# Both column halves of the mLSTM output projection at hand at once, and its products taken in another order

## The chip, the cores and the metric

One core of a Trainium2 chip runs the whole program. The metric is the device time of one execution in microseconds (us). The engines are PE (TensorE, matrix products), DVE (VectorE), ACT (ScalarE), POOL (GpSimd) and SP (SyncE, which issues most DMAs). They run side by side, each through its own list of instructions in order, and wait for one another by semaphores.

## The reference

A small decoder trunk in float32: 512 tokens of width 1024, one mLSTM layer, then one sliding-window attention layer. Each layer ends with the same three steps. What matters here:

```python
def mlstm_mixer(x, w_in, b_ig, b_fg, head_g, w_out):
    ...
    h = h.reshape(B, S, D_MODEL).astype(x.dtype)
    return (jax.nn.sigmoid(o) * h) @ w_out

    for i in range(DEPTH):
        ...
        x = layer_norm(DEEPNORM_ALPHA * x + mix, mix_ln_g[i], mix_ln_b[i])
        x = layer_norm(DEEPNORM_ALPHA * x + squared_relu_mlp(x, mlp_w_up[i], mlp_w_down[i]), mlp_ln_g[i], mlp_ln_b[i])
        x = x + jax.nn.sigmoid(x @ ple_w_gate[i] + ple_b_gate[i]) * (p[i] @ ple_w_proj[i])
```

The product with `w_out` (1024 x 1024) and the layer norm behind it are the place of the change.

## The kernel before

**Numbers.** Every float32 operand of a product is split into a rounded high part and the rest. `split` (L75) does it: ACT copies the raw tile into `whi` (L76), DVE subtracts to get `wlo` (L77). A product is then three matmuls, high by high, high by low, low by high (`mm3`, L88 to L90).

**Tiling.** The 512 tokens are four tiles of 128, t0 to t3. The width of 1024 is eight k-blocks of 128 on the contracted side and two halves of 512 columns on the output side. One output block (a token tile by a half) takes 8 x 3 = 24 matmuls into one bank of PSUM, the accumulator memory. In this part of the program five banks are called `mm` and three `tp` (for transposes and the small products of the heads).

**Weights.** `load_w` (L79) takes three raw buffers and six pairs `whi`, `wlo` from `wpool`. SP issues the load of a raw tile as soon as DVE has subtracted from the tile that lay there before. Since one half of `w_out` needs four pairs, six pairs hold one half and a part of the next.

**mLSTM.** Four heads follow one another. `mlstm_scores(3)` and `mlstm_out(3)` end with a chain of small steps: products on PE into `tp`, copies on ACT (L414), statistics on DVE, a power on POOL (L138), the scaling of `num` (L428, L431), eight transposes on PE (L435) and the split into `YH`, `YL` (L436, L437). Head 3 fills the last two k-blocks of `YH`, `YL`; k-blocks 0 to 5 are there long before.

**Output projection.** `xstat_mix` (L162) takes half 0 of all four token tiles, then half 1 of all four. Behind each block, `add_res` (L159) adds the scaled residual `res[t]` on DVE and `bn_stats` (L173) takes statistics. Behind half 1 of a token tile comes `ln_finish`: a power on POOL (L138), two passes on DVE over 1024 columns (L145, L146), eight transposes on PE (L129), the split into `XH` on ACT (L133) and `XL` on DVE (L134), and the scaling by alpha on ACT (L149).

**After it.** The first four tiles of the MLP's up projection (L608) take columns 0 to 255 of `XH`, `XL`, so they need token tiles t0 and t1 alone at first. The second layer's output projection (L953 to L966) is code of its own with the same `add_res` and `ln_finish`.

**What sets the order.** The program is written in the order of the source, but the framework's scheduler then simulates the program and sorts each engine's instructions by readiness and priority. So a change at one place can move instructions far behind it as well. The pools reuse memory tile by tile: `mid` (the residual) and the new pool of the change lie partly where the heads' pool `pa` lay.

Of the kernel before, what the change touches and what calls it, by code (L numbers as in the profile page):

```python
# [11 lines left out]
F32R = mybir.dt.float32r  # L12
# [7 lines left out]
P = 128  # L20
S = 512
NT = S // P
D = 1024
KD = D // P
# [21 lines left out]
def yoco_kernel(ctx: ExitStack, tc: tile.TileContext, A: dict, out: bass.AP):  # L46
    nc = tc.nc
    V, ACT, PE, GP = nc.vector, nc.scalar, nc.tensor, nc.gpsimd

    def pool(name, bufs=1, stack=ctx, **kw):  # L50
        return stack.enter_context(tc.tile_pool(name=name, bufs=bufs, **kw))

    base = pool("base")
    wpool = pool("wpool")
# [10 lines left out]
    def mm_bank():  # L65
        return bank("mm")
# [8 lines left out]
    def split(raw, n, hi, lo, eng=V):  # L75
        ACT.copy(hi, raw)  # L76
        eng.tensor_sub(lo, raw, f32(hi))  # L77

    def load_w(src, n, eng=V):  # L79
        raw = wpool.tile([P, 1024], F32, tag="raw", name="wraw", bufs=3)  # L80
        hi = wpool.tile([P, 1024], F32R, tag="whi", name="whi", bufs=6)
        lo = wpool.tile([P, 1024], F32R, tag="wlo", name="wlo", bufs=6)
        nc.sync.dma_start(raw[:, :n], src)
        split(raw[:, :n], n, hi[:, :n], lo[:, :n], eng)
        return hi, lo

    def mm3(o, lh, ll, rh, rl, start, stop):
        PE.matmul(o, lh, rh, start=start, stop=False)  # L88
        PE.matmul(o, lh, rl, start=False, stop=False)  # L89
        PE.matmul(o, ll, rh, start=False, stop=stop)  # L90
# [18 lines left out]
    def tsl(t):  # L109
        return slice(t * P, (t + 1) * P)  # L110
# [29 lines left out]
    def ln_finish(t, st, g, b, mlp_next=True):  # L140
        mv = small.tile([P, 2], F32, tag="mv", name="mv")
        V.bn_aggr(mv, st)
        rs = small.tile([P, 1], F32, tag="rs", name="rs")
        rsqrt_eps(rs, mv[:, 1:2], 1)
        V.scalar_tensor_tensor(res[t], res[t], mv[:, 0:1], g, ALU.subtract, ALU.mult)  # L145
        V.scalar_tensor_tensor(res[t], res[t], rs, b, ALU.mult, ALU.add)  # L146
        transpose_in(res[t], t, XH, XL)
        if mlp_next:
            ACT.mul(res[t], res[t], ALPHA)  # L149
            if t >= 2:  # L150
                r = res[t - 2][:, 512:]
                V.tensor_sub(r, r, res[t][:, 512:])

    def add_res(t, half, ps, alpha):
        r = res[t][:, half * 512:(half + 1) * 512]
        if alpha is None:
            V.tensor_add(r, r, ps)
        else:
            V.scalar_tensor_tensor(r, r, alpha, ps, ALU.mult, ALU.add)  # L159
        return r  # L160

    def xstat_mix(wname, xh, xl, alpha, g, b):  # L162
        sts = [small.tile([P, 2, 6], F32, tag="lst", name="lst", bufs=4) for _ in range(NT)]
        for half in range(2):
            w = [load_w(A[wname][half, c], 1024) for c in range(4)]
            for t in range(NT):
                ps = mm_bank()
                for k in range(KD):
                    wh, wl = w[k // 2]
                    sl = slice((k % 2) * 512, (k % 2 + 1) * 512)  # L170
                    mm3(ps, xh[:, k, tsl(t)], xl[:, k, tsl(t)], wh[:, sl], wl[:, sl], k == 0, k == KD - 1)
                r = add_res(t, half, ps, alpha)
                V.bn_stats(sts[t][:, half, :], r)  # L173
                if half == 1:
                    ln_finish(t, sts[t], g, b)

    sin = base.tile([P, NT, HALF], F32, name="sin")
    cos = base.tile([P, NT, HALF], F32, name="cos")
# [296 lines left out]
    g, b = bcast(A["mix_ln_g"][0]), bcast(A["mix_ln_b"][0])  # L475
# [327 lines left out]
    w = [load_w(A["w_kv"][0, c], 1024) for c in range(4)]  # L803
# [5 lines left out]
    for t in range(NT):  # L809
        ps = proj512(t, w)  # L810
# [109 lines left out]
    w = load_q(0)  # L920
# [125 lines left out]
```

## Time and profile before

| what | value |
|---|---|
| three executions | 1200.96, 1202.63, 1204.96 us, median 1202.63 |
| profiled execution, own time | 1205.24 us |
| its span, first to last instruction | 1203.5 us |
| DVE busy | 877.7 us, 73% of the span |
| ACT busy | 584.4 us, 49% |
| POOL busy | 95.7 us, 8% |
| HBM read | 119.34 MB, 103 GB/s over the span |

The profile is of one execution. A line of its timeline gives start, duration, engine, source line, operation, what is written and read, the shape, the count when several follow one another, and in brackets how long the engine sat idle before it and what ended that wait. The granted clock is the share of full speed that PE was given in a stretch. Times below are counted from the start of the span. The mLSTM's output projection lies at about 168 to 220 us, the attention of the second layer at 650 to 775 us and its output projection at 765 to 800 us.

### The profile page before, as it was taken

How to read it: one execution, taken by the hardware profiler on the slowest of the kernel's cores; microseconds unless marked ns; L12 is line 12 of the kernel's file. 1: busy time of each engine (PE TensorE's matmuls, PEld its weight loads, DVE VectorE, ACT ScalarE, POOL GpSimd, SP SyncE). 2: the span in 40 equal slices, each digit the busy share in tenths (PEclk: the TensorE clock that was granted, in tenths of full speed). 3: DMA queues.
4: the chain of work that ended last, by engine and by line, in shares of the span. 5: the costliest groups of instructions: out<-in, count | busy, mean ns of one | idle time of the engine just before them, and what ended most of it. 6: DMA issues, size and time to landing. Idle time of an engine off the chain costs nothing.

```text
span 1203.5 us, 15661 instructions
## 1 busy us (share of the span) xinstructions
PE 1181.0 (98%) x5918; PEld 1004.2 (83%) x5918; DVE 877.7 (73%) x1454; ACT 584.4 (49%) x1015; POOL 95.7 (8%) x190
## 2 busy tenths in 40 slices
PE   9999999999999999999999999999999999999998
PEld 8899988888888888888788998789888888888877
DVE  6556466877488499599785988586857848959974
ACT  4445551565463463564344655346645536346431
POOL 1011021100000000001201332110000000000100
PEclk9999999999999999999999999989999999999999
DMA  7322227214405316115242211451350440621411
GB/s 229 119 92 71 85 74 280 71 36 140 140 1 179 101 37 192 52 53 175 80 175 88 71 37 36 152 198 36 95 168 18 140 141 1 192 88 36 157 54 52
DMA packets 35995, 124.54 MB, mean 103 GB/s; under 512 B 4096, under 2 KB 4880, under 8 KB 35920
## 3 DMA queue, kind: packets, MB, share of 16 engines
q1 hardware_dynamic: 33840, 116.46, 29.8%
q0 software_dynamic: 2080, 7.09, 1.8%
q8 instruction: 46, 0.75, 0.2%
q14 instruction: 29, 0.24, 0.1%
HBM read 119.34 MB, written 4.19 MB: 103 GB/s over the span
## 4 chain that ended last, share of the span: by engine, by line
PE 88%; DVE 6%; ACT 2%; DMA 2%; issue 1%; SPq 0%; POOL 0%; ACTq 0%; DVEq 0%
PE mm L90 28%; PE mm L89 28%; PE mm L88 28%; PE tp L129 1%; DVE wlo L77 1%; ACT pr L883 1%; ACT whi L76 1%; PE tp L88 1%; PE tp L89 1%; PE tp L90 1%; DMA wraw<-in_w_vo_dram 1%; DVE sc L869 1%; DVE QS L853 0%; DVE smax L870 0%; DMA res<-spill 0%
## 5 line engine op out<-in xcount | busy, mean ns | idle before, releaser
L77 DVE TENSOR_TENSOR wlo<-wraw,whi 128x1024 fp32r<-128x1024 f32 (+1 forms) x168 | 204.2, 1218 | 126.4 <-ACT whi L76 125.4
L76 ACT CAST whi<-wraw 128x1024 fp32r<-128x1024 f32 (+1 forms) x168 | 173.7, 1037 | 243.2 <-PE mm L90 133.1
L89 PE MATMUL mm<-XL,whi 128*128 128x512 f32 (+1 forms) x640 | 237.7, 372 | 1.7 <-DVE XL L134 1.7
L88 PE MATMUL mm<-XH,whi 128*128 128x512 f32 (+1 forms) x640 | 236.2, 371 | 1.9 <-ACT ot L265 1.3
L90 PE MATMUL mm<-XH,wlo 128*128 128x512 f32 (+1 forms) x640 | 237.1, 371 | 0.0
L88 PE MATMUL mm<-whi,XH 128*128 128x512 f32 (+2 forms) x424 | 146.1, 346 | 3.9 <-DVE q L843 2.2
L89 PE MATMUL mm<-wlo,XH 128*128 128x512 f32 (+2 forms) x424 | 145.1, 343 | 0.0
L90 PE MATMUL mm<-whi,XL 128*128 128x512 f32 (+2 forms) x424 | 144.4, 343 | 0.0
L89 PEld LDWEIGHTS mm<-XL,whi 128*128 128x128 f32 x640 | 122.5, 191 | 21.6 <-DVE XL L134 1.9
L88 PEld LDWEIGHTS mm<-XH,whi 128*128 128x128 f32 x640 | 121.6, 191 | 22.3 <-ACT ot L265 1.7
L90 PEld LDWEIGHTS mm<-XH,wlo 128*128 128x128 f32 x640 | 122.5, 191 | 19.9
L76 ACT CAST whi<-rb 128x1024 fp32r<-128x1024 f32 x80 | 84.0, 1051 | 100.6 <-PE mm L89 56.4
L77 DVE TENSOR_TENSOR wlo<-rb,whi 128x1024 fp32r<-128x1024 f32 x80 | 97.6, 1224 | 38.9 <-ACT whi L76 38.9
L88 PEld LDWEIGHTS mm<-whi,XH 128*128 128x128 f32 x424 | 79.9, 189 | 13.0 <-DVE q L843 3.9
L89 PEld LDWEIGHTS mm<-wlo,XH 128*128 128x128 f32 x424 | 80.1, 189 | 7.7 <-issue 1.5
L90 PEld LDWEIGHTS mm<-whi,XL 128*128 128x128 f32 x424 | 80.1, 189 | 6.5 <-issue 0.8
L89 PE MATMUL mm<-wlo,S23h 128*128 128x512 f32 x128 | 50.7, 396 | 0.0
L89 PE MATMUL mm<-wlo,S4Ah 128*128 128x512 f32 x128 | 50.6, 395 | 0.0
L88 PE MATMUL mm<-whi,S23h 128*128 128x512 f32 x128 | 50.6, 395 | 0.0
L88 PE MATMUL mm<-whi,S4Ah 128*128 128x512 f32 x128 | 50.6, 395 | 0.0
L90 PE MATMUL mm<-whi,S4Al 128*128 128x512 f32 x128 | 50.3, 396 | 0.0
L637 DVE TENSOR_TENSOR res<-res,mm 128x512 f32<-128x512 f32 x72 | 48.8, 685 | 1.4 <-PE mm L90 1.0
(354 smaller groups left out, 2231.3 us busy)
## 6 DMA issues: line engine op xcount, KB each, us to landing
wraw<-in_w_up_dram SPq DMA_DIRECT2D x64, 512.0 KB, 3.6
rb<-in_w_down_dram SPq DMA_DIRECT2D x48, 512.0 KB, 4.4
wraw<-in_w_down_dram SPq DMA_DIRECT2D x16, 512.0 KB, 3.5
wraw<-in_w_gate_dram SPq DMA_DIRECT2D x16, 512.0 KB, 3.7
wraw<-in_w_vo_dram SPq DMA_DIRECT2D x18, 412.0 KB, 3.2
wraw<-in_w_qk_dram SPq DMA_DIRECT2D x8, 512.0 KB, 4.7
wraw<-in_w_out_dram SPq DMA_DIRECT2D x8, 512.0 KB, 3.8
wraw<-in_w_q_dram SPq DMA_DIRECT2D x8, 512.0 KB, 3.9
```

The lines of the kernel that those rows point to most:

```text
L76: ACT.copy(hi, raw)
L77: eng.tensor_sub(lo, raw, f32(hi))
L88: PE.matmul(o, lh, rh, start=start, stop=False)
L89: PE.matmul(o, lh, rl, start=False, stop=False)
L90: PE.matmul(o, ll, rh, start=False, stop=stop)
L129: PE.transpose(pt[:, tsl(j)], src[:, tsl(b + j)], ident)
L637: V.tensor_add(r[:, h], r[:, h], bank)
L869: V.copy_predicated(cur, mk, prev)
L883: ACT.activation(pt_[:, par, pr, :], scs[pr][:, par, :], AF.Exp, scale=ASCALE, bias=nm[:, par, pr:pr + 1], accum_out=sm[:, par, pr:pr + 1])
```

## The change

`load_w` can take its `hi` and `lo` tiles from a pool handed to it. `xstat_mix` opens such a pool (`wroom0`, four pairs `xhi`, `xlo`), loads half 0 into `wpool` and half 1 into the new pool, and then goes through the eight blocks in a list of its own: half 0 of t0, t1, t2, then half 1 of t0 and t1, half 0 of t3, half 1 of t2 and t3. The loads, splits and matmuls are the same in number and shape.

```diff
-    def load_w(src, n, eng=V):
+    def load_w(src, n, room=None):
         raw = wpool.tile([P, 1024], F32, tag="raw", name="wraw", bufs=3)
-        hi = wpool.tile([P, 1024], F32R, tag="whi", name="whi", bufs=6)
-        lo = wpool.tile([P, 1024], F32R, tag="wlo", name="wlo", bufs=6)
+        hi, lo = (room.tile([P, 1024], F32R, tag=f"x{x}", name=f"x{x}", bufs=4) if room else
+                  wpool.tile([P, 1024], F32R, tag=f"w{x}", name=f"w{x}", bufs=6) for x in ("hi", "lo"))
         nc.sync.dma_start(raw[:, :n], src)
-        split(raw[:, :n], n, hi[:, :n], lo[:, :n], eng)
+        split(raw[:, :n], n, hi[:, :n], lo[:, :n])
         return hi, lo
...
-        for half in range(2):
-            w = [load_w(A[wname][half, c], 1024) for c in range(4)]
-            for t in range(NT):
-                ps = mm_bank()
-                for k in range(KD):
-                    wh, wl = w[k // 2]
...
+        wctx = ExitStack()
+        room = pool("wroom0", stack=wctx, side="right", reuse_waits="tile")
+        w = [[load_w(A[wname][half, c], 1024, room if half else None) for c in range(4)] for half in range(2)]
+        for t, half in ((0, 0), (1, 0), (2, 0), (0, 1), (1, 1), (3, 0), (2, 1), (3, 1)):
+            ps = mm_bank()
+            for k in range(KD):
+                wh, wl = w[half][k // 2]
...
+        wctx.close()
```

Lines from L164 on stand two lines further down in the changed kernel. The scheduler's lists show the move at three places.

On PE, where the eight transposes of head 3 (`tp_1704`, `tp_1711`) stand. In the kernel before, `mm_1762`, `mm_1789`, `mm_1816`, `mm_1843` are half 0 of t0 to t3 and `mm_1894` is half 1 of t0:

```order
L90 MATMUL mm_1894<-whi_1877,YL_98 128x512
L88 MATMUL mm_1894<-whi_1883,YH_97 128x512
L435 MATMUL tp_1704<-ident_66,num_1633 128x128 x4
L435 MATMUL tp_1711<-ident_66,num_1633 128x128 x4
L89 MATMUL mm_1894<-wlo_1884,YH_97 128x512
L90 MATMUL mm_1894<-whi_1883,YL_98 128x512
```

And in the changed kernel, where `mm_1789`, `mm_1816`, `mm_1843` are half 0 of t0, t1, t2, `mm_1870`, `mm_1919` half 1 of t0, t1, and `whi_1760` holds the k-blocks of head 3:

```order
L89 MATMUL mm_1843<-wlo_1755,YH_97 128x512
L90 MATMUL mm_1843<-whi_1754,YL_98 128x512
L437 MATMUL tp_1704<-ident_66,num_1633 128x128 x4
L437 MATMUL tp_1711<-ident_66,num_1633 128x128 x4
L88 MATMUL mm_1789<-whi_1760,YH_97 128x512
L89 MATMUL mm_1789<-wlo_1761,YH_97 128x512
L88 MATMUL mm_1816<-whi_1760,YH_97 128x512
```

Before, four blocks of k-blocks 0 to 5 and thirteen matmuls of a fifth stand ahead of the transposes, and five more matmuls that need nothing of head 3 behind them. Now three blocks stand ahead, and the first row behind the transposes reads what they yield. The splits of the other half (`xhi`) stand behind the cast of `YH` on ACT.

On DVE, behind the last block's `add_res` (`mm_2042`, half 1 of t3), in the kernel before. The normalisation of t0 and t1 (L145, L146 on `res0`, `res1`) stands well ahead of this place:

```order
L159 SCALAR_TENSOR_TENSOR res3_1725<-res3_1725,mm_2042 128x512
L77 TENSOR_TENSOR wlo_2375<-wraw_2373,whi_2374 128x1024
L134 TENSOR_TENSOR XL_65<-tp_1977,XH_64 128x4x128
L146 SCALAR_TENSOR_TENSOR res2_1724<-res2_1724,rs_2021,bc_1732 128x1024
L77 TENSOR_TENSOR wlo_2422<-wraw_2420,whi_2421 128x1024
```

In the changed kernel the last block is `mm_2045`; `tp_1904`, `tp_1911` are transposes of t0, `tp_1953`, `tp_1960` of t1:

```order
L159 SCALAR_TENSOR_TENSOR res3_1725<-res3_1725,mm_2045 128x512
L142 BN_AGGR mv_2022<-lst_1736 128x2
L174 BN_STATS lst_1737<-res3_1725 128x6
L137 TENSOR_SCALAR rs_2024<-mv_2022 128x1
L145 SCALAR_TENSOR_TENSOR res2_1724<-res2_1724,mv_2022,bc_1730 128x1024
L134 TENSOR_TENSOR XL_65<-tp_1904,XH_64 128x4x128
L142 BN_AGGR mv_2072<-lst_1737 128x2
L134 TENSOR_TENSOR XL_65<-tp_1911,XH_64 128x4x128
L146 SCALAR_TENSOR_TENSOR res2_1724<-res2_1724,rs_2024,bc_1732 128x1024
L134 TENSOR_TENSOR XL_65<-tp_1953,XH_64 128x4x128
L137 TENSOR_SCALAR rs_2074<-mv_2072 128x1
L145 SCALAR_TENSOR_TENSOR res3_1725<-res3_1725,mv_2072,bc_1730 128x1024
```

Before, the two splits of t0 (L134) stood ahead of the last block's row and only those of t1 behind it. Now all four stand behind it (that of `tp_1960` next after these rows), with both passes of t2 and the first of t3 between them. On PE the transposes of t0 and t1 stand behind the last block too, where before those of t0 stood inside it.

On DVE in the second layer's output projection, which the diff does not touch, in the kernel before (`mm_7387` and `mm_7437` are half 1 of t2 and t3):

```order
L157 TENSOR_TENSOR res2_7181<-res2_7181,mm_7387 128x512
L146 SCALAR_TENSOR_TENSOR res1_7180<-res1_7180,rs_7367,bc_7189 128x1024
L964 BN_STATS lst_7193<-res2_7181 128x6
L134 TENSOR_TENSOR XL_65<-tp_7323,XH_64 128x4x128
L134 TENSOR_TENSOR XL_65<-tp_7330,XH_64 128x4x128
L142 BN_AGGR mv_7414<-lst_7193 128x2
L137 TENSOR_SCALAR rs_7416<-mv_7414 128x1
L145 SCALAR_TENSOR_TENSOR res2_7181<-res2_7181,mv_7414,bc_7187 128x1024
L77 TENSOR_TENSOR wlo_7537<-wraw_7535,whi_7536 128x1024
L77 TENSOR_TENSOR wlo_7543<-wraw_7541,whi_7542 128x1024
L146 SCALAR_TENSOR_TENSOR res2_7181<-res2_7181,rs_7416,bc_7189 128x1024
```

And in the changed kernel, where `mm_7391` is half 1 of t2:

```order
L146 SCALAR_TENSOR_TENSOR res1_7184<-res1_7184,rs_7371,bc_7193 128x1024
L157 TENSOR_TENSOR res2_7185<-res2_7185,mm_7391 128x512
L966 BN_STATS lst_7197<-res2_7185 128x6
L134 TENSOR_TENSOR XL_65<-tp_7327,XH_64 128x4x128
L134 TENSOR_TENSOR XL_65<-tp_7334,XH_64 128x4x128
L142 BN_AGGR mv_7418<-lst_7197 128x2
L137 TENSOR_SCALAR rs_7420<-mv_7418 128x1
L145 SCALAR_TENSOR_TENSOR res2_7185<-res2_7185,mv_7418,bc_7191 128x1024
L77 TENSOR_TENSOR wlo_7541<-wraw_7539,whi_7540 128x1024
L146 SCALAR_TENSOR_TENSOR res2_7185<-res2_7185,rs_7420,bc_7193 128x1024
L77 TENSOR_TENSOR wlo_7547<-wraw_7545,whi_7546 128x1024
```

One split of a weight (L77) now stands behind the second pass of t2 (L146) instead of ahead of it. The attention between the two projections is dealt out in another order on PE, DVE, ACT and POOL as well.

More of the change, by code (lines that the diff above doesn't have):

```diff
@@ L163, in xstat_mix @@
         sts = [small.tile([P, 2, 6], F32, tag="lst", name="lst", bufs=4) for _ in range(NT)]
-        for half in range(2):
-            w = [load_w(A[wname][half, c], 1024) for c in range(4)]
-            for t in range(NT):
-                ps = mm_bank()
-                for k in range(KD):
-                    wh, wl = w[k // 2]
[L170 to L175, printed above, removed]
+        wctx = ExitStack()
[5 more added lines that the diff above has]
+                wh, wl = w[half][k // 2]
+                sl = slice((k % 2) * 512, (k % 2 + 1) * 512)
+                mm3(ps, xh[:, k, tsl(t)], xl[:, k, tsl(t)], wh[:, sl], wl[:, sl], k == 0, k == KD - 1)
+            r = add_res(t, half, ps, alpha)
+            V.bn_stats(sts[t][:, half, :], r)
+            if half == 1:
+                ln_finish(t, sts[t], g, b)
+        wctx.close()
     sin = base.tile([P, NT, HALF], F32, name="sin")
```

## The prediction

> **What bounds the kernel now.** First the page: the busy shares and the chain that ended last.
>
> ```profile
> PE 1181.0 (98%) x5918; PEld 1004.2 (83%) x5918; DVE 877.7 (73%) x1454; ACT 584.4 (49%) x1015; POOL 95.7 (8%) x190
> ...
> PE 88%; DVE 6%; ACT 2%; DMA 2%; issue 1%; SPq 0%; POOL 0%; ACTq 0%; DVEq 0%
> ```
>
> PE is the bound: 98% busy and 88% of the chain. The change leaves every matmul in place, so it can only move the little time in which PE waits or runs slowly. The timeline of PE around the end of the first output projection shows where that is.
>
> ```profile
> 219.67 1.04 PE L129 MATMUL tp<-ident,res 128*128 128x128 f32 x8
> 221.30 0.74 PE L88 MATMUL mm<-XH,whi 128*128 128x256 f32 x4 [0.59 <-ACT XH L133]
> 223.77 0.39 PE L89 MATMUL mm<-XL,whi 128*128 128x256 f32 x1 [1.74 <-DVE XL L134]
> ```
>
> Eight transposes hold PE for 0.79 us when a matmul follows them (192.86 to 193.65 in the rows of (a)), so here they are through by 220.46 and PE stands 0.84 us. Matmuls of 256 columns step by about 0.12 (31, some transposes among them, fill 3.4 us in the third row of the next view), so four are through by 221.78; PE stands 1.99 us more, for DVE. Together **2.83 us**. Then comes a price that no wait shows, in the windows view of 3.4 us each (busy time of PE, PEld, DVE, ACT, POOL, then the granted clock).
>
> ```profile
> 220.90:224.30 3.40, 1.27 (x8) 1.06 (x9) 3.40 (x6) 2.74 (x4) 0.00 (x0) 1.00 0.40 131
> 224.30:227.70 3.40, 3.40 (x18) 3.40 (x18) 3.40 (x10) 0.00 (x0) 0.00 (x0) 0.50 0.58 190
> 227.70:231.10 3.40, 3.40 (x31) 3.40 (x31) 3.07 (x6) 2.22 (x4) 1.45 (x1) 1.00 0.30 117
> 797.70:801.10 3.40, 1.58 (x13) 1.17 (x10) 3.40 (x4) 2.40 (x4) 0.00 (x0) 1.00 0.76 246
> 801.10:804.60 3.50, 2.68 (x13) 2.68 (x14) 3.50 (x6) 2.68 (x4) 0.00 (x0) 0.51 0.62 211
> 804.60:808.00 3.40, 3.40 (x18) 3.40 (x18) 2.71 (x6) 0.01 (x1) 1.45 (x1) 0.50 0.54 154
> 1149.30:1152.70 3.40, 2.26 (x13) 1.15 (x11) 3.40 (x5) 1.59 (x4) 0.00 (x0) 1.00 0.44 154
> 1152.70:1156.10 3.40, 3.40 (x18) 2.83 (x16) 3.40 (x10) 1.87 (x2) 1.15 (x1) 1.00 0.00 0
> ```
>
> After a window with PE busy 1.27 or 1.58 us the next one ran at half speed; after 2.26 it didn't. A slow window with 2.68 busy was followed by another slow one, a slow window fully busy by a fast one. A slow window full of matmuls costs half of 3.4: **1.7 us**. So the first projection's end costs 2.83 + 1.7 = 4.5 us, and that of the second layer, at 798, more.
>
> **The change, part by part.** *(a) The cover of head 3.* The change takes away what PE had to do while head 3 finished.
>
> ```profile
> 181.50 0.28 PE L90 MATMUL tp<-vh,sl 128*128 128x258 f32 x1
> 182.09 0.40 PE L88 MATMUL mm<-whi,YH 128*128 128x512 f32 x1
> ...
> 192.63 0.39 PE L88 MATMUL mm<-whi,YH 128*128 128x512 f32 x1
> 192.86 1.03 PE L435 MATMUL tp<-ident,num 128*128 128x128 f32 x8
> 193.65 0.48 PE L89 MATMUL mm<-wlo,YH 128*128 128x512 f32 x1
> ```
>
> ```profile
> 183.87 1.01 POOL L138 TENSOR_TENSOR hv<-hv,nhalf 128x4 f32<-128x4 f32 x1 [5.44 <-DVE hv L137]
> ```
>
> ```profile
> 176.28 2.43 DVE L400 TENSOR_TENSOR sl<-dt,sh 128x256 fp32r<-128x256 f32 x1 [1.49 <-ACT sh L399]
> ...
> 186.54 1.23 DVE L431 TENSOR_TENSOR num<-num,ot 128x1024 f32<-128x1024 f32 x1
> ```
>
> ```profile
> 173.60 1.28 ACT L429 ACT_TABLE_LOAD   x1
> ...
> 193.50 1.07 ACT L436 CAST YH<-tp 128x512 fp32r<-128x512 f32 x2 [2.43 <-PE tp L435]
> ```
>
> The 46 matmuls from 182.09 to 192.63 step by 10.54 / 45 = 0.234 us. PE's products of head 3 end at 181.6 and the chain through DVE and POOL makes `num` ready at 186.54 + 1.23 = 187.77. Before, 48 matmuls lay behind 181.6, and the transposes came at 192.86, late and without a wait. Now the order has 16 there (one more stood ahead: 181.7): PE is through at 181.7 + 16 x 0.234 = 185.45 and stands until about 187.92, **2.47 us**. Does `num` come earlier or later? On ACT a second table load (1.28) now delays the last 128 columns of head 3's scores, but DVE no longer sits in the 2.43 us subtraction meanwhile, and PE reaches the product that needs them only at about 180.2; so I leave 187.77. Behind the transposes (0.79) the first row needs `YH`: ACT starts 0.64 after the first transpose and takes 0.58, so PE stands from 188.71 to 189.2, **0.49**. Sum 2.96, ends 2.5 and 3.5.
>
> Is that wait also a slow window? On the trace's grid of windows (220.9 less ten times 3.41 is 186.8; the grid is another in each execution) PE is busy for 1.0 us of transposes and 0.7 of matmuls, 1.75 in all. The nearest row is 1.58, which slowed. So **+1.7**, ends 0 and 1.7. In the Trainium skill the page "TensorE: Matmul & The Clock Gate" (section "Why this matters for your kernels") asks only that PE has no idle gap above about 3 us; by it the wait of 2.47 would cost no clock, and the time would be that of R2 below. This trace speaks against it: waits of 1.99 and 0.84 us with four matmuls between them were enough.
>
> *(b) Weights of half 1.* The splits move behind the `YH` casts, at 189.6 on ACT, one per 1.05 us; PE wants the first after 18 matmuls (193.4) and a fourth only 47 later. The last raw tile waits on SP behind the four loads of `res` and for DVE's first split of half 1 (192); it lands some 4 us later (page part 6: 3.8), 8 us ahead of need. The loads of `res` start earlier than before. Cost nothing, hidden by the 36 matmuls of half 1; without that cover 1 to 4 us.
>
> *(c) The end of the projection.* 138 matmuls are left at 189.2: 32.3 us, so the transposes of t0 start at T = 221.5 (223.2 with the slow window). What stands behind T follows from these rows.
>
> ```profile
> 200.50 1.29 DVE L159 SCALAR_TENSOR_TENSOR res<-res,mm 128x512 f32<-128x512 f32 x2 [5.10 <-PE mm L90]
> 205.81 1.88 DVE L173 BATCH_NORM_STATS2 lst<-res 128x6 f32<-128x512 f32 x3
> 209.16 1.27 DVE L145 SCALAR_TENSOR_TENSOR res<-res,mv,bc 128x1024 f32<-128x1024 f32 x1
> 230.70 1.28 DVE L134 TENSOR_TENSOR XL<-tp,XH 128x512 fp32r<-128x512 f32 x2
> ```
>
> ```profile
> 217.80 1.07 ACT L133 CAST XH<-tp 128x512 fp32r<-128x512 f32 x2 [0.55 <-PE tp L129]
> 218.75 1.07 ACT L149 ACTIVATE res<-res 128x1024 f32<-128x1024 f32 x1
> ```
>
> In a row DVE takes 0.6 per step of 512 columns and 1.2 per pass of 1024. ACT: the two casts of t0 from T + 0.64 to 1.6, the scaling to 2.6, the cast of t1 to 3.2. PE: 12 transposes to T + 1.2, then it stands **2.0** for that cast; four matmuls to 3.7, four transposes to 4.1. The transposes of t2 wait for DVE: `add_res` and statistics from T + 0.25, first pass, two splits of t0, second pass, small steps 0.3, that is 0.25 + 1.2 + 1.2 + 1.2 + 1.2 + 0.3 = 5.35: **1.3** more. The next four need a free `tp` bank, the split of t1 at 6.0: **0.25**. Sum 3.55 where 2.83 was: the wait isn't removed, since both passes of t2 now run behind the last block. Together with (a): 2.96 + 3.55 - 2.83 = **+3.7 us** of standing (ends 2.5 and 5).
>
> Slow windows here: with T = 223.2 the window 224.3 to 227.7 has PE busy about 1.4, near 1.27, so the next is slow; it has about 2.5 busy, near the slow row of 2.68, so one more follows. Of the first only the stretch from 229.5 is full of work: 1.0, then 1.7. With (a) 1.7 + 2.7, against 1.7 before: **+2.7** (ends -1.7, none at all, and +2.7).
>
> *(d) The second layer's projection.* The scheduler moved it, as the third pair of rows shows.
>
> ```profile
> 797.12 1.03 PE L129 MATMUL tp<-ident,res 128*128 128x128 f32 x8
> 799.68 0.63 PE L129 MATMUL tp<-ident,res 128*128 128x128 f32 x4 [1.52 <-DVE res L146]
> 800.06 0.74 PE L88 MATMUL mm<-XH,whi 128*128 128x256 f32 x4
> 801.92 1.11 PE L129 MATMUL tp<-ident,res 128*128 128x128 f32 x4 [1.12 <-DVE XL L134]
> ```
>
> ```profile
> 795.98 2.36 DVE L77 TENSOR_TENSOR wlo<-wraw,whi 128x1024 fp32r<-128x1024 f32 x2
> 798.25 1.28 DVE L146 SCALAR_TENSOR_TENSOR res<-res,rs,bc 128x1024 f32<-128x1024 f32 x1
> ```
>
> PE stands from 797.91 to 799.68 and from 800.53 to 801.92: 3.16 us. From 779 on DVE is nearly without a gap. With one split less ahead of it (2.36 / 2 = 1.18) the second pass of t2 ends at 798.35 instead of 799.5: PE stands 0.45. The next four transposes need a bank that DVE frees after that split (1.15) and one more (0.6), at 800.1: 1.3. Then 13 matmuls of t0 and t1 follow at once. 1.75 in place of 3.16: **-1.4** (ends -2.5 and +1.4). PE is then busy about 2.1 in the window from 797.7, near the 2.26 that didn't slow; the two slow windows, 5.8 us of half speed behind 801.92, go: **-2.9** (ends -2.9 and 0).
>
> *(e) The attention between.* Its order is shuffled on four engines.
>
> ```profile
> 650.00:770.00 120.00, 113.69 (x830) 104.73 (x829) 92.29 (x241) 63.24 (x223) 37.03 (x88) 1.00 0.14 44
> ```
>
> PE stands 120 - 113.7 = 6.3 us there, in many short pieces. A shuffle could remove some or add as much; nothing in the rows says which. I take **0**, ends -3 and +3, half of it.
>
> **Sum:** 3.7 + 2.7 - 1.4 - 2.9 + 0 = **+2.1 us** on the profiled execution's own 1205.24, so 1207.3. That execution lies 2.6 above the median of the three (1202.63), about one and a half slow windows; I put the same difference on the median: **1204.7 us**.
>
> **The rivals.**
> - *(R1) Slower by half a per cent: (d) doesn't happen.* The gain of (d) hangs on DVE being full from 779 and on `res` landing when it did. If the shuffled attention leaves DVE later at 777, the pass of t2 ends at 799.5 or later again, PE waits as before and both slow windows stay. Then 3.7 + 2.7 = +6.4: 1209.0. It decides from a delay of 1.2 us on. For it: the first wait of DVE there is for a DMA (3.75 us for `res` from the spill), which any reorder of loads can shift; against: those loads keep their order.
> - *(R2) The wait of (a) costs no clock.* Then T is 221.5, the window from 224.3 is slow but holds little work (0.4), that from 227.7 is slow and full (1.7): 2.1 against 1.7 before, and 3.7 + 0.4 - 4.3 = -0.2: 1202.4. It is what the page of the Trainium skill named in (a) would give. For it: 1.75 us busy lies between 1.58 and 2.26, and on another grid the wait is cut in two by a window's edge; the three times before lie 4.0 us apart, which would fit windows that differ. Against: 1.58 is the nearer row.
> - *(R3) The wait at the end really goes,* if DVE is through with t0 to t2 before the last block: then 2.96 + 1.7 - 2.83 - 1.7 - 4.3 = -4.2: 1198.4. Against it: between half 1 of t1 and the last block PE has 56 matmuls, 13.1 us, and the order gives DVE there eight steps of 0.6, two splits of 1.2 and the four passes of t0 and t1, 12 us; the first pass of t2 stands behind the last block in any case.
>
> **How the numbers follow.** A run tells 0.3% (3.6 us) from no change. Forecast 0.45, R1 0.25, R2 0.18, R3 0.12. The forecast with (e)'s ends goes from 1201.7 to 1207.7, above 1206.2 in about a sixth of its cases. So slower 0.25 + 0.07 = 0.32, faster 0.12 (R3), same 0.56. The range runs from 1199.5, leaving most of R3 out, to 1209.5, R1 and a little of (e).
>
> **What would show it.** Right: PE stands 2 to 3 us just ahead of the `num` transposes, released by DVE's last product; then about 0.5 for `YH`; after the last block three waits of 2.0, 1.3 and 0.3; granted clock half near 190 and 228; at 798 waits of 0.5 and 1.3 at full clock. Wrong: `num` ready before 186, a wait for `xhi` or `res` (then (b) has a price), DVE through with t2's passes before the last block, or attention windows with PE standing under 3 or over 9 us.

## The result: 0.95% slower, and the profile after

The changed kernel takes 1214.51 us (median of six, 1210.25 to 1215.82) where the kernel before takes 1202.07 beside it (median of six): ratio **1.0095, interval 1.0081 to 1.0108**. The forecast was 1204.7 us and "no change". The profiled execution of the changed kernel took 1214.29 us, its span 1212.6, so 9.05 us more than the one of before. That one, at 1205.24 us, lies 3.2 us above the median of its kernel, so the rows below show less than the loss in the medians. Medians and ratios here leave out the few executions in a slow state that strikes any kernel (one of split_room: 1296.78 us at a granted clock of 0.85), and split_room, whose only profile fell into it, has no rows.

PE's total work did not move; the page of the changed kernel still has it at 98%:

```profile
PE 1182.3 (98%) x5918; PEld 1005.3 (83%) x5918; DVE 876.6 (72%) x1454; ACT 585.7 (48%) x1016; POOL 96.1 (8%) x190
```

So the 9 us are waits and slow clock, and the first question is where. Two rows for each kernel serve as milestones: the first and last score matmul of the attention, and the moment at which the second layer's residual is fetched back. In the views of single tiles (count, shortest/median/longest ns, first and last start) the kernel before has

```profile
L864 PE MATMUL sc<-KH,QS x64: 277/282/387, 662.4 to 753.8; 128*128 128x256 f32 x64
L950 SPq DMA_DIRECT2D res<-spill x4: 382/383/847, 771.8 to 773.2; - x4
```

and the changed one

```profile
L866 PE MATMUL sc<-KH,QS x64: 277/286/387, 665.0 to 759.3; 128*128 128x256 f32 x64
L952 SPq DMA_DIRECT2D res<-spill x4: 383/546/1357, 779.4 to 781.1; - x4
```

The edited projection lies 440 us back when the first score matmul runs, and only 2.6 us have been lost by then. Between the first and the last score matmul 2.9 more go (94.3 us in place of 91.4), the reload is 7.6 late, the end 9.05. **Most of the loss is made in code that the diff doesn't touch.** The windows by stage (busy time of PE, PEld, DVE, ACT, POOL, granted clock) say the same. Before, the second projection's stage reads

```profile
770.00:830.00 60.00, 56.75 (x347) 51.08 (x346) 40.94 (x58) 24.74 (x42) 7.10 (x6) 0.94 0.53 193
```

and after, it and the attention ahead of it

```profile
650.00:770.00 120.00, 111.00 (x806) 103.41 (x805) 89.07 (x239) 59.51 (x219) 35.78 (x86) 0.97 0.16 49
770.00:830.00 60.00, 54.97 (x318) 47.76 (x317) 39.64 (x57) 23.42 (x37) 8.37 (x8) 0.94 0.48 175
```

PE stands 9.0 us of the attention's 120 (6.3 before), and its clock is no longer full there.

**The first projection** waited nearly as forecast. PE's timeline after the change:

```profile
187.62 1.29 PE L437 MATMUL tp<-ident,num 128*128 128x128 f32 x8 [2.41 <-DVE num L433]
221.97 1.47 PE L129 MATMUL tp<-ident,res 128*128 128x128 f32 x12
225.16 0.74 PE L88 MATMUL mm<-XH,whi 128*128 128x256 f32 x4 [1.72 <-ACT XH L133]
225.74 0.60 PE L129 MATMUL tp<-ident,res 128*128 128x128 f32 x4
227.44 1.17 PE L129 MATMUL tp<-ident,res 128*128 128x128 f32 x8 [1.10 <-DVE res L146]
```

The wait for `num` is 2.41 us (forecast 2.47), the waits after the last block 1.72 and 1.10 (forecast 2.0 and 1.3). The wait for `YH`, forecast at 0.49, does not show.

**The attention** waits in new places. Rows of DVE, ACT and PE near 670 us after the change:

```profile
667.18 1.22 DVE L77 TENSOR_TENSOR wlo<-wraw,whi 128x1024 fp32r<-128x1024 f32 x1
668.87 0.76 DVE L872 TENSOR_REDUCE smax<-sc 128x2 f32<-128x256 f32 x2
670.12 0.16 DVE L877 SCALAR_TENSOR_TENSOR anm<-smax,nsink 128x4 f32<-128x4 f32 x1
670.36 1.28 ACT L885 ACT_TABLE_LOAD   x1 [1.12 <-DVE anm L877]
672.52 0.38 PE L866 MATMUL sc<-KH,QS 128*128 128x256 f32 x1 [1.63 <-ACT pr L885]
```

The next score needs a bank that the exponentials on ACT must first read; these wait for the maximum on DVE and a table load, and PE's list now has score after score there. In the kernel before, products of the query projection stand between the scores, and the longest wait of PE from 662 to 676 us is 0.59 us.

**The second projection** has a stall of 4.2 us that is new. SP, DVE and PE after the change:

```profile
779.39 3.07 SPq L952 DMA_DIRECT2D res<-spill  x4
785.91 0.69 DVE L157 TENSOR_TENSOR res<-res,mm 128x512 f32<-128x512 f32 x1 [5.42 <-DMA res<-spill]
788.49 0.69 DVE L157 TENSOR_TENSOR res<-res,mm 128x512 f32<-128x512 f32 x1 [1.17 <-DMA res<-spill]
789.82 0.67 DVE L157 TENSOR_TENSOR res<-res,mm 128x512 f32<-128x512 f32 x1
790.55 0.80 PE L88 MATMUL mm<-whi,QS 128*128 128x512 f32 x1 [4.18 <-DVE res L157]
```

and in the kernel before:

```profile
777.36 0.69 DVE L157 TENSOR_TENSOR res<-res,mm 128x512 f32<-128x512 f32 x1 [3.75 <-DMA res<-spill]
778.69 0.67 DVE L157 TENSOR_TENSOR res<-res,mm 128x512 f32<-128x512 f32 x1
779.61 0.69 DVE L157 TENSOR_TENSOR res<-res,mm 128x512 f32<-128x512 f32 x1 [0.24 <-DMA res<-spill]
```

PE goes on when the add of t0's second half has emptied its bank. Before, that add stands second on DVE; now it stands third, behind t1's add, which waits for a reload of its own. DVE's lists, before and after:

```
res0_7179<-res0_7179,mm_6956        res0_7183<-res0_7183,mm_6960
res0_7179<-res0_7179,mm_7289        res1_7184<-res1_7184,mm_7036
res1_7180<-res1_7180,mm_7032        res0_7183<-res0_7183,mm_7293
```

**The clock.** The windows of 3.4 us around all stretches of the span at half clock, after the change. In each group the window in which PE had little work comes first:

```profile
184.89:188.30 3.41, 1.00 (x8) 0.71 (x7) 2.55 (x5) 0.01 (x1) 1.75 (x11) 1.00 0.63 215
188.30:191.71 3.41, 3.40 (x11) 2.41 (x10) 2.56 (x4) 3.34 (x5) 0.00 (x0) 0.50 0.26 100
669.58:672.99 3.41, 1.46 (x11) 1.07 (x11) 1.99 (x7) 2.62 (x9) 1.05 (x4) 1.00 0.40 144
672.99:676.40 3.41, 3.41 (x19) 3.41 (x18) 2.73 (x9) 2.14 (x11) 0.00 (x0) 0.50 0.02 5
758.32:761.73 3.41, 1.83 (x11) 1.20 (x10) 2.54 (x10) 2.07 (x11) 0.94 (x2) 1.00 0.00 0
761.73:765.15 3.42, 3.42 (x17) 3.32 (x16) 2.00 (x6) 2.35 (x11) 1.46 (x3) 0.50 0.02 5
785.63:789.04 3.41, 0.74 (x4) 0.27 (x2) 1.93 (x3) 1.04 (x1) 0.00 (x0) 1.00 1.03 399
789.04:792.45 3.41, 1.90 (x5) 1.52 (x6) 3.38 (x6) 0.00 (x0) 0.00 (x0) 0.50 1.01 405
792.45:795.87 3.42, 3.42 (x10) 2.65 (x9) 3.42 (x8) 0.00 (x0) 1.53 (x1) 0.50 1.03 422
```

Two of the five slow windows lie in the attention, at 1.7 us each; the kernel before has three in all (one at 224, two at 801) and none there.

### The profile page after: what moved, and what is told of

Same layout as the page of the kernel before. It is cut to its first block, busy times and chain, and to the rows that moved or that the text cites. A ratio compares the mean times of both kernels' runs of the same rounds, so it can differ in the third digit from the quotient of the medians.

```text
span 1212.6 us, 15658 instructions
## 1 busy us (share of the span) xinstructions
PE 1182.3 (98%) x5918; PEld 1005.3 (83%) x5918; DVE 876.6 (72%) x1454; ACT 585.7 (48%) x1016; POOL 96.1 (8%) x190
## 5 line engine op out<-in xcount | busy, mean ns | idle before, releaser
L77 DVE TENSOR_TENSOR wlo<-wraw,whi 128x1024 fp32r<-128x1024 f32 (+1 forms) x164 | 199.2, 1217 | 126.8 <-ACT whi L76 125.6
L76 ACT CAST whi<-wraw 128x1024 fp32r<-128x1024 f32 (+1 forms) x164 | 169.7, 1036 | 224.5 <-PE mm L90 110.6
L77 DVE TENSOR_TENSOR wlo<-rb,whi 128x1024 fp32r<-128x1024 f32 x80 | 97.5, 1223 | 39.0 <-ACT whi L76 39.0
```

## Experiments

**Theory 1:** the loss is mostly the scheduler's other order of attention and second projection. **Theory 2:** the change itself costs it, through its room, its transfers or its order of blocks, wherever it shows.

The two can be told apart because the scheduler sorts by a simulated clock of its own: a warm-up matmul more or less at the program's start shifts that clock, and the lists downstream come out another way. Orders that are equal row for row on all engines from the end of the first MLP on have one letter here: A is that of the changed kernel, B that of the kernel before, C and K two others. The experiments compare kernels with the same letter, or kernels with the same first projection under two letters. Each kernel has as many warm-ups (5 to 9) as give it its letter. Every ratio is against the kernel before, run beside it.

| kernel | order | median us | ratio (interval) | score matmuls in its profile, us |
|---|---|---|---|---|
| changed | A | 1214.51 | 1.0095 (1.0081 to 1.0108) | 665.0 to 759.3 |
| five_warm | A | 1215.34 | 1.0099 (1.0083 to 1.0114) | 666.1 to 760.5 |
| old_blocks_order_a | A | 1216.69 | 1.0113 (1.0098 to 1.0128) | 667.0 to 759.9 |
| split_room_order_a | A | 1208.59 | 1.0037 (1.0024 to 1.0050) | 661.4 to 754.3 |
| six_warm | B | 1207.91 | 1.0035 (1.0022 to 1.0049) | 665.5 to 757.0 |
| six_hold | B | 1205.16 | 1.0021 (1.0008 to 1.0034) | 666.1 to 757.7 |
| own_landing | B | 1204.96 | 1.0013 (1.0000 to 1.0027) | 663.9 to 755.4 |
| split_room | B | 1200.48 | 0.9978 (0.9965 to 0.9992) | none |
| five_warm_before | C | 1205.48 | 1.0021 (1.0009 to 1.0032) | 663.3 to 754.8 |
| keep_before | K | 1201.39 | 0.9990 (0.9980 to 0.9999) | 662.4 to 753.9 |
| keep_after | K | 1205.17 | 1.0020 (1.0011 to 1.0030) | 666.9 to 758.4 |
| keep_hold_after | K | 1203.60 | 1.0008 (0.9999 to 1.0017) | 664.2 to 755.7 |
| keep_old | K | 1208.62 | 1.0045 (1.0028 to 1.0061) | 669.8 to 761.3 |
| keep_old_hold | K | 1208.61 | 1.0040 (1.0026 to 1.0054) | 667.6 to 759.1 |
| keep_own_landing | K | 1203.73 | 1.0007 (0.9995 to 1.0018) | 663.0 to 754.6 |
| keep_old_landing | K | 1207.66 | 1.0032 (1.0019 to 1.0046) | 666.1 to 757.7 |
| keep_split_room | K | 1199.14 | 0.9958 (0.9941 to 0.9975) | 659.4 to 751.0 |
| keep_old_split_room | K | 1202.43 | 0.9989 (0.9978 to 1.0001) | 664.2 to 755.7 |

### The order downstream

```diff
-    warm_up(7)
+    warm_up(6)     # six_warm; five_warm and five_warm_before: warm_up(5)
```

```diff
-    for t, half in ((0, 0), (1, 0), (2, 0), (0, 1), (1, 1), (3, 0), (2, 1), (3, 1)):
+    for t, half in ((0, 0), (1, 0), (2, 0), (3, 0), (0, 1), (1, 1), (2, 1), (3, 1)):     # old_blocks_order_a
```

> The changed kernel with 6 instead of 7 idle warm-up matmuls at its start and nothing else. That one matmul less shifts the clock of the scheduler that sorts the instructions, so that from the end of the first MLP on (the last 3080 rows of TensorE, and the other engines likewise) the order is that of the kernel before, row for row, while the first projection keeps the change's order. Theory 1 (the loss is made downstream, by the other order of attention and second projection): 1204.6 us, +0.2% against the kernel before, the +2.6 us being what the first projection has lost by the first score matmul (662.4 to 665.0 us in the two profiles); the spill reload is issued near 774 us, no 4 us stall of TensorE near 786, no 1.8 us wait for pr near 670. Theory 2 (the change itself, its room in memory, its transfers or its waits, costs the time wherever it shows): 1213 to 1216 us, +1.0%.

> The changed kernel with 5 warm-up matmuls: one less than in six_warm, but here the order downstream is again that of the changed kernel, row for row. This is the control on the warm-up. Theory 1: 1214 us, +0.95%, as the changed kernel, and the first score matmul where six_warm has it within 0.5 us. Theory 2 says the same of the time here; if the number of warm-ups itself mattered (theory 3), five_warm would stand beside six_warm instead, within 1 us.

> The first projection in its old order of blocks (all four first halves, then all four second halves), with both halves' weights in hand in the new room, and 8 warm-ups, with which the order downstream is that of the changed kernel, row for row. Theory 1: the first projection comes out as before (first score matmul near 662.5 us), and the loss downstream is there in full, 1202.1 + 6.5 = 1208.5 us (1207 to 1211), +0.55%, with the late spill reload and the 4 us stall. Theory 2 (the blocks' order in the first projection makes the loss): 1202 us, no change. If the room alone made it: 1212 to 1215.

> The kernel before with 5 warm-up matmuls and nothing else: its first projection is untouched, and its order downstream is a third one, neither that of before nor of the changed kernel. Theory 1 (the order downstream is worth several us by itself): anything from 1199 to 1212 us, and more than 2 us away from 1202.1 is likely; the first score matmul stays at 662.4 within 0.5 us. Theory 2: 1202.1 within 0.3%, as nothing of the change is in it.

One warm-up matmul takes the loss from 0.95% to 0.35% (1207.91 us; 1204.6 was expected). The stage rows of six_warm against the kernel before (113.69 and full clock in the attention):

```profile
650.00:770.00 120.00, 113.67 (x843) 105.31 (x842) 92.13 (x242) 62.27 (x222) 36.44 (x87) 1.00 0.16 50
770.00:830.00 60.00, 56.96 (x360) 50.68 (x358) 43.40 (x61) 26.91 (x43) 7.83 (x8) 1.00 0.54 193
```

With the order of before, the attention's PE time is that of before to 0.02 us, with the change's first projection ahead of it (its list there differs from the changed kernel's in a few places, as a table below shows). PE's wait for the residual there is

```profile
782.43 0.50 PE L88 MATMUL mm<-whi,QS 128*128 128x512 f32 x1 [0.44 <-DVE res L157]
```

0.44 in place of 4.18 us. All profiles agree: the four with order A have 111.0 us of PE work in the attention's window and wait 3.8 to 4.2 us for the residual; the four with order B have 113.5 to 113.7 us, and three of them wait 0.4 to 0.6 us. In the fourth, six_hold's, which is the slowest of that kernel's twelve executions (1209.78 us), the first reload reached DVE 7.4 us after its issue (5.6 in the kernel before) and PE waited 2.44 us. five_warm, with two warm-ups less than the changed kernel and its order A, stands where that kernel stands, so the number of warm-ups is not what counts. Theory 2 is out for the larger part of the loss: **the order downstream costs 0.64%** (1.0099 against 1.0035).

five_warm_before, without any of the change, came out 0.21% slower than the kernel before by such a shift: 1.0021, within the wide range that was expected. Its first score matmul was expected within 0.5 us of before's and came 0.9 us later.

old_blocks_order_a missed its mark upward (1208.5 expected, 1216.7 measured). Its wait for `num` is gone, as expected, but it waits at the end of the first projection instead:

```profile
223.24 2.46 PE L129 MATMUL tp<-ident,res 128*128 128x128 f32 x12 [4.71 <-DVE mv L142]
```

So theory 1 leaves a rest: 0.35% in six_warm come from the first projection, and the old order of blocks, with weights in the new room, is no better.

### What the first projection loses, and the residual kept

Two edits, shown by their main lines: the residual rows stay in memory through the attention, in a pool of their own, so that nothing is written out and read back (keep); and VectorE may split the first four `w_up` chunks only behind t1's last normalising pass (hold).

```diff
-        res[:] = [mid[0].tile([P, D], F32, name=f"res{t}") for t in range(NT)]
...
+    pres = pool("pres", stack=rctx, side="left", reuse_waits="tile")
+    res[:] = [pres.tile([P, D], F32, name=f"res{t}") for t in range(NT)]
...
-                    nc.sync.dma_start(spill[t], res[t])
...
-    for t in range(NT):
-        nc.sync.dma_start(res[t], spill[t])
```

```diff
+        normed[t] = V.scalar_tensor_tensor(res[t], res[t], rs, b, ALU.mult, ALU.add).ins
...
+                with tc.issue_after(normed[1]) if i == 0 else nullcontext():
+                    w = [load_w(A["w_up"][i, j], 1024) for j in range(j0)]
```

> six_warm with one edge more: VectorE's splits of the first four w_up chunks may be issued only behind the second token tile's last normalising pass (before it, the changed kernel has all four of them ahead of the second halves' adds of tiles 0 and 1). Order downstream as in six_warm and before, row for row. Theory 1 (the end of the first projection waits because VectorE does the next layer's weights first): the two waits of 1.36 and 1.82 us after the last block shrink to under 1 us together, the first score matmul comes 2 to 3 us sooner than in six_warm (665.5), and the time is 1205.3 us (+0.15% against before; 1204 to 1206). The 2.6 us wait for num near 185 stays. Theory 2 (the waits belong to the new order of blocks, two second halves being normalised at the end): the time of six_warm, 1207.9, within 0.1%. A turn for the worse (1209) would say that the w_up parts are then late for the MLP.

> The kernel before, with the residual rows kept in memory through attention in place of being written out and read back (the four stores and the four reloads are gone, the same values are used). Theory 1 (the stall of the second projection is the wait for those reloads, which are issued only when attention's memory comes free): no wait of VectorE for a DMA there, and the 0.8 us wait of TensorE near 778 is gone. The order of attention is a new one (a fourth), so its stage may come out at 12 to 18 us of waits. 1196 to 1204 us with an order as good as that of before, likeliest 1201; 1205 to 1208 with one as bad as the changed kernel's.

> The same with the changed kernel and 6 warm-ups: downstream of the first MLP its order is row for row that of keep_before, so the two differ in the first projection alone. Theory 1: 3 to 4.5 us slower than keep_before (what six_warm lost against before: +0.25 to +0.4%), and no 4 us stall near 786. Theory 2 (the change costs 1% whatever the order downstream): 12 us slower than keep_before.

> keep_after with the edge of six_hold: the splits of the first four w_up chunks behind the second tile's last normalising pass; the order downstream is that of keep_before and keep_after, row for row. Theory 1: 2 to 3 us faster than keep_after, so within 0.5 to 2 us of keep_before; if it is the best of all it is because the waits at the end of both projections are gone: 1200 us. Theory 2: as keep_after.

keep_before is 0.1% faster than the kernel before, and no add there waits for a reload. keep_after is 0.30% slower than keep_before, with equal lists downstream and no reload to wait for: a second measure of the first projection's own loss, which agrees with six_warm's 0.35%. The hold is worth 0.12 to 0.14% where it was tried, with intervals that overlap, less than the 2 to 3 us expected. The profiles do not settle it: the first score matmul came 2.7 us sooner in keep_hold_after than in keep_after, which had one slow window more ahead of it, and no sooner in six_hold (666.1).

> keep_after with the old order of blocks (all four first halves, then all four second halves), both halves' weights still in hand in the new room; 6 warm-ups; downstream row for row the order of keep_before and keep_after. It differs from keep_before by the weights in hand, from keep_after by the order of blocks. Theory 1: with four blocks in front the 2.6 us wait for num near 185 is gone (three blocks are too little cover for the fourth head); but VectorE still has the four w_up splits ahead of the second halves' adds, so the wait at the end of the projection is the 4 to 5 us that old_blocks_order_a showed: 1204 to 1206 us, as keep_after (1205.2). Theory 2 (the order of blocks makes the loss of the first projection): 1201.4 us, as keep_before.

> keep_old with the w_up splits held behind the second tile's last normalising pass (and 5 warm-ups, with which the order downstream is again that of keep_before). Theory 1: neither the wait for num nor the long wait at the end: within 1.5 us of keep_before either way (1200 to 1202.9), 2 to 5 us faster than keep_old and 1 to 3 us faster than keep_hold_after. If the order of VectorE did not matter, it would stand with keep_old.

With the old order of blocks the new room costs more, not less: keep_old is 0.55% slower than keep_before, 0.25% slower than keep_after (1208.62 us; 1204 to 1206 was expected). The order of blocks is therefore not the culprit. And the hold does nothing there. DVE's row in keep_old_hold tells why:

```profile
211.82 0.69 DVE L160 SCALAR_TENSOR_TENSOR res<-res,mm 128x512 f32<-128x512 f32 x1 [5.02 <-PE mm L90]
```

DVE sits idle for 5 us until PE is through with t0's second half. It was not VectorE's order that was late but PE's block. The theory behind the hold fell, and PE's lists gave the next one. Of the 192 matmuls of the projection, counted in them:

| kernel | ahead of the `num` transposes | still to come when half 1 of t0 / t1 is done |
|---|---|---|
| before, keep_before | 85 | 72 / 48 |
| changed | 54 | 61 / 56 |
| six_warm, keep_after | 54 | 54 / 49 |
| keep_old | 72 | 34 / 29 |
| own_landing, keep_own_landing | 54 | 76 / 53 |
| keep_old_landing | 72 | 55 / 38 |
| split_room, keep_split_room | 78 | 77 / 72 |
| keep_old_split_room | 84 | 72 / 48 |

In the changed kernel no second-half block can begin before head 3 is through, because all of its weights are in the new room: the first is cast at 189.4 us, where the kernel before has cast two chunks of that half by 172.6. The last of them comes later still, through three shared landing buffers (issued at 191.8 us, cast at 195.4), so that three blocks end close together: the third stands 48 matmuls before the end.

### Where the second half's weights lie

```diff
-        raw = wpool.tile([P, 1024], F32, tag="raw", name="wraw", bufs=3)
+        raw = (room.tile([P, 1024], F32, tag="xraw", name="xraw", bufs=4) if room else
+               wpool.tile([P, 1024], F32, tag="raw", name="wraw", bufs=3))     # own_landing and the other two
```

> The changed kernel with 7 warm-ups and one edit: the second half's four weight chunks land in four buffers of the new room, in place of the ring of three that all weights share. Downstream its order is row for row that of before (and of six_warm). In the changed kernel the last of those chunks comes late (its split is issued behind the first halves' adds), so the scheduler lets the blocks of tiles 0, 1 (second half) and 3 (first half) run up to it and finish all three together, 48 groups before the end; with landing buffers they finish one after the other. Theory 1 (the late chunk bunches the normalising at the end): the waits after the last block shrink to under 1.5 us in all; the 2.6 us wait for num near 185 stays, as three blocks stand in front; 1204 to 1206 us, 2 to 4 us faster than six_warm. Theory 2 (the order of blocks as written makes the end wait): 1207.9 us, as six_warm.

> The same edit in keep_after, with 7 warm-ups; order downstream that of keep_before and keep_after. Theory 1: 2 to 4 us faster than keep_after (1205.2), so 1201 to 1203. Theory 2: 1205.2 us.

> The same edit in keep_old (old order of blocks, four first halves in front), 7 warm-ups, order downstream that of keep_before. Neither the wait for num (four blocks of cover) nor the bunching (the four second halves end 17 or 21 groups apart). Theory 1: the best of these kernels: 0 to 2 us under keep_before, 1199.5 to 1201.5. Theory 2 (weights in hand cost something by themselves, as keep_old's +0.55% against keep_before might say): 1206 to 1209 us, as keep_old.

Landing buffers of its own give the changed kernel 0.22% back (own_landing against six_warm), 0.13% with the residual kept (1203.73 us; 1201 to 1203 was expected); the intervals of both pairs overlap. The waits after the last block came to 1.66 us in own_landing, where under 1.5 was expected. The old order was expected to be the best of all with them and isn't (1207.66 us for 1199.5 to 1201.5); its rows of SP and PE show what lies under all of this:

```profile
191.12 2.65 SPq L84 DMA_DIRECT2D xraw<-in_w_out_dram  x4
201.80 2.08 PE L89 MATMUL mm<-xhi,YH 128*128 128x512 f32 x4 [5.62 <-ACT xhi L76]
```

The room lies in the memory of the heads' pool. What goes there is issued at 191 us, when head 3 is done, and PE stands 5.6 us for it. (In this kernel the loads themselves go there; in the changed kernel only the casts do.) In the kernel before two pairs of the common ring take the first two chunks of half 1 long before. "Both halves at hand" was less at hand than before.

```diff
-        w = [[load_w(A[wname][half, c], 1024, room if half else None) for c in range(4)] for half in range(2)]
+        w = [[load_w(A[wname][half, c], 1024, room if half and c > 1 else None) for c in range(4)] for half in range(2)]
```

> The changed kernel with the first two chunks of the second half in the two pairs that the common ring has free (as in the kernel before), and only the last two in the new room; 9 warm-ups, with which the order downstream is that of before, row for row. The room lies in the heads' memory, so what is in it cannot be cast before the fourth head is through; with two chunks in the ring, 78 matmuls stand ahead of the num transposes in the order (54 in the changed kernel), and 72 groups follow the end of tile 1's second block (48 in the changed kernel). Theory 1 (the new room itself made the loss of the first projection, by coming too late): no wait for num near 185, under 1.5 us of waits after the last block; first score matmul 662 to 663.5 us, time 1201.5 to 1203.5 us, level with before; two warm-ups more may cost up to 0.5 us. Theory 2 (weights in hand or the order of blocks cost something by themselves): 1205 to 1208 us, as own_landing or six_warm.

> The same edit in keep_after, 7 warm-ups, order downstream that of keep_before and keep_after. Theory 1: level with keep_before or better, 1199.5 to 1202 us (keep_after 1205.2); it would be the best of all kernels here. Theory 2: 1203.7 (as keep_own_landing) to 1205.2 us.

> keep_old with the same edit: the old order of blocks, the first two chunks of the second half in the ring, 7 warm-ups, order downstream that of keep_before. On TensorE this is the order of keep_before in the first projection too, but for the last two chunks' place. Theory 1: 1201 to 1203 us, level with keep_before (keep_old had 1208.6). Theory 2: 1205 to 1208 us.

> split_room with 5 in place of 9 warm-ups; with these the order downstream is that of the changed kernel, row for row. The first projection is that of split_room. Theory 1 (the order downstream costs about 0.65% by itself, as five_warm against six_warm): 1201.0 + 7.5 = 1208.5 us (1206.5 to 1210.5), with the late spill reload, the wait of 3 to 5 us near 785 and slow clock windows near 670, 760 or 790. Theory 2 (the other order only hurts together with the late room): 1201 to 1203 us.

With two of the four chunks in the ring, the change's order of blocks is **0.22% faster than before** where it was 0.35% slower (split_room against six_warm, both order B), and with the residual kept 0.42% faster: keep_split_room, at 1199.14 us, is the best kernel of the study and faster than both. Its first projection, in PE's timeline and in the stage row:

```profile
191.90 1.03 PE L436 MATMUL tp<-ident,num 128*128 128x128 f32 x8
193.17 0.50 PE L88 MATMUL mm<-whi,YH 128*128 128x512 f32 x1 [0.24 <-ACT YH L437]
```

```profile
175.00:250.00 75.00, 74.70 (x450) 65.75 (x449) 56.98 (x108) 34.06 (x57) 13.70 (x17) 1.00 0.46 162
```

The transposes of head 3 come without a wait, 0.24 us is the only wait of that stretch, and PE is busy 74.70 of 75 us where the kernel before and the changed kernel have

```profile
175.00:250.00 75.00, 72.67 (x432) 64.22 (x431) 53.79 (x104) 31.57 (x54) 10.62 (x17) 0.98 0.44 161
175.00:250.00 75.00, 69.76 (x414) 61.10 (x413) 53.04 (x104) 31.69 (x51) 9.39 (x18) 0.98 0.44 148
```

keep_old_split_room shows what the new order of blocks is worth once the room is split: with the old order the kernel is level with keep_before (0.9989 and 0.9990, as expected), with the new one it is 0.31% faster (0.9958).

split_room_order_a then puts the good first projection ahead of order A: 1.0037, 0.59% slower than split_room, with a 3.8 us wait for the residual again. The first projections of these two kernels agree in the counts of the table above. The price is nearly that between five_warm and six_warm (0.64%), so the downstream loss stands by itself. The two parts add up to the result: about 0.35% from the first projection, which is 0.57% lost by the late room less 0.22% that the rest of the change gains, and about 0.6% from order A.

## Why the prediction was wrong

Counted between the milestones of the two profiles, the changed kernel lost 2.6 us up to the first score matmul, where (a) to (c) had put 6.4; 2.9 between the first and the last score matmul, where (e) had put 0; and about 3.5 behind it, where (d) had put a gain of 4.3. The first part came out smaller than forecast, so part of the miss was cancelled by luck.

- **(a) Cover of head 3: right in size.** PE stood 2.41 us (2.47 forecast), and the window behind it was slow (0.50 at 188.30). The rule of the Trainium skill that was weighed there ("TensorE: Matmul & The Clock Gate", section "Why this matters for your kernels": no idle gaps above about 3 us) would have left the clock alone; the window with a 2.41 us wait and 1.00 us of work was followed by a slow one. Rival R2, in which that wait costs no clock, did not happen in this execution. In five_warm it did, in the way that R2 named: the same wait of 2.41 us lay across a window's edge (2.14 and 2.03 us of work in the two), and no slow window followed. In keep_own_landing none followed a wait of 2.17 us with 1.70 us of work in the window. So the 1.7 us is a matter of where the grid falls.
- **(b) Weights of half 1 at cost nothing: wrong, though no wait showed it.** PE never waited for `xhi` in the changed kernel, and the casts came at 189.4 us (189.6 forecast); for that reason (b) looked free. But that the room is late is why (a) has 54 matmuls of cover and why (c) has three blocks ending together. With half of the room's chunks in the ring both waits went (as the profiles of keep_split_room and split_room_order_a show), and 0.57% with them (split_room against six_warm). The forecast priced the arrival of the weights at the place where they are used, and took the order of PE around it as given. The sum is not off by this, since (a) and (c) hold its price.
- **(c) End of the projection: the waits right, the clock not.** The waits were 1.72 and 1.10 us for 2.0 and 1.3; the third, put at 0.25, didn't come. Two slow windows, 2.7 us, were added behind them, and this profile has neither. The forecast had a window with about 1.4 us of work there; the grid fell otherwise and cut the waits in two:

```profile
222.43:225.84 3.41, 1.69 (x15) 1.45 (x14) 3.41 (x8) 2.50 (x4) 1.45 (x1) 1.00 0.88 322
225.84:229.26 3.42, 2.32 (x20) 1.99 (x19) 3.42 (x6) 2.70 (x5) 1.16 (x1) 1.00 0.60 237
```

  keep_after has a slow window at 229, so this too differs between executions. PE's standing in the stage rose by 2.9 us (3.7 forecast), its slow windows by none (one before, one after; 2.7 us forecast). The two pairs of medians put the whole at 0.30 to 0.35%, 3.6 to 4.2 us, where (a) and (c) with their clock had 6.4.
- **(d) Second projection: a gain at its end, and a larger loss ahead of it.** In the view of groups from 775 to 825 us the transposes at its end now wait 0.9 us in all, where the rows of before had 1.52 and 1.12 us, and the two slow windows behind them went:

```profile
L129 PE MATMUL tp<-ident,res 128*128 128x128 f32 x32 | 4.6, 275 | 0.9 <-DVE XL L134 0.5 <-DVE res L146 0.4
```

  Whether (d)'s reason made this gain is not shown: PE came there later, and the two slow windows went in six_warm, too, whose list is that of before. But the reload of the residual, issued 7.6 us later and taken by DVE in another order, made PE stand 4.18 us and brought two slow windows of its own. The forecast used the rows of before for everything ahead of the normalising; rival R1 named the danger ("any reorder of loads can shift") and set it against the order of the loads alone. That order did stay; what moved was the end of the attention: its last product starts at 779.3 us after the change and at 772.5 before, and the reloads, which go where the attention's tiles lay, are issued with it.
- **(e) The attention at 0, ends -3 and +3: the step that failed, together with what (d) took from it.** PE's standing there rose from 6.3 to 9.0 us, which the ends of 3 us allowed for, and two slow windows added 3.4. That a reordered attention could also bring slow windows, and delay and reorder the reloads behind it, was not priced: (d) kept the rows of before up to the normalising, and PE stood 4.18 us there. Three orders (B, C, K) take 91.4 to 91.6 us from the first score matmul to the last, order A 92.9 to 94.4: the shuffle was not a zero with a small spread but a draw in which this one was poor.

Which of the changed rows of order A costs how much was not tried apart.

## What to carry to other kernels

Where a scheduler sorts the whole program, an edit buys a new order for everything behind it, and here that draw (0.6%) was larger than the edit (0.35%). Measure an edit between kernels with equal lists downstream; a neutral shift at the start, such as one warm-up matmul, finds such pairs. And a new pool is only as early as the memory it lies in: look at who held that memory last before calling its contents at hand.

## What the hardware showed that was not expected

The same two waits at the end of the second projection, about 1.5 and 1.1 us, cost two slow windows in one execution and none in another. In the profile of before the window from 797.7 with 1.58 us of work was followed by two at half clock; in six_warm, where the lists are the same,

```profile
800.58:803.99 3.41, 1.74 (x14) 1.32 (x12) 3.41 (x4) 2.25 (x4) 0.00 (x0) 1.00 0.75 251
803.99:807.41 3.42, 2.50 (x21) 2.50 (x22) 3.42 (x6) 2.85 (x4) 0.00 (x0) 1.00 0.65 204
```

the full clock stayed, and the stage from 770 to 830 us had a clock of 1.00 in place of 0.94. Of the other two profiles with these lists, six_hold has 1.27 us of work in that window and one slow window behind it, own_landing 1.71 us and none. In the changed kernel a window with 1.69 us of work (from 222.43) kept the full clock and one with 1.83 us (from 758.32) was followed by a slow one, so no sharp limit comes out of PE's busy time. A single profile can therefore carry up to two slow windows at one place, 3.4 us, that the next execution need not have.
